# HGRN heads: state increments of a direction in a row into two PSUM banks, then the states, then the products with the states

## The chip, the cores and the metric

The kernel runs on one core of one Trainium2 chip. The metric is the device time of one execution in microseconds (us); before the change three runs took 1531.09, 1536.82 and 1536.36 us, median 1536.36. About 0.5% (7.7 us) is what a measurement of this kernel can tell from no change.

## The reference, cut to what matters

The program is a two-layer encoder over 512 tokens of width 1024. The even layer projects its input, mixes half of the channels by a bidirectional gated linear recurrence (HGRN2, 4 heads of 128) and the other half by RWKV-7 (8 heads of 64), concatenates, projects out, and runs a convolutional feed-forward; the odd layer mixes by Fourier transforms and a convolution. Only the HGRN recurrence is touched. Per head and direction the reference computes, chunk after chunk:

```
def step(state, xs):
    q_n, k_n, v_n, dec_n = xs
    o_n = jnp.einsum('bchd,bhdv->bchv', q_n, state)
    state = state * dec_n[..., None] + jnp.einsum('bchd,bchv->bhdv', k_n, v_n)
    return state, o_n
_, o_inter = lax.scan(step, state0, xs)
return (o_intra + jnp.moveaxis(o_inter, 0, 1))
...
o = _gla_chunk_forward(q4, k_f, i4, lf_f) + flip(_gla_chunk_forward(flip(q4), flip(k_b), flip(i4), flip(lf_b)))
o = _rmsnorm(o, norm_g) * jax.nn.silu(heads(g))
```

The kernel cuts the 512 tokens into 8 chunks of 64. The increment of the state, the product of keys and values of one chunk, doesn't depend on the state; the next state and the product of queries with the state do.

## The kernel before

The even layer is a list of stages, PLAN (lines 53 to 64 of the kernel): for each pair p of RWKV heads `pair`, `unit0`, `unit1` (one for each direction), `inv0`, `inv1`, `chain0`, `chain1`, `post`; for each HGRN head `proj` (its part of the input projection) and `hgrn`; then `ada` (modulation vectors, products L207), and `out 0`, `out 1`, the parts of the output projection whose inputs are complete (blocks of nine 128x512 products, L136 to L138, added up by VectorE in L870). The last part of the output projection (L1058 to L1062, `ab_out2`) needs the results of the last HGRN head and of the last `post`.

Each unit of RWKV has a triangular solve on VectorE, 62 short instructions one after the other (L555, L557), on tiles that exist once (`L`, `xi`, lines 542 and 543); its result is copied by L601 and L602, goes to DRAM and back through SyncE's queue (L603, L612, L614), and is then used by `inv` (products L620, L630, L641, L647, additions L649) and `chain` (seven steps: two small products L658, a copy by VectorE L659, a copy by ScalarE L660; then sixteen products L666). There are eight units and so eight solves. `post` normalises the sum of the two directions: on VectorE L672, L681, L682, L684, L688, on ScalarE L686 and the logarithm and exponential behind L689, on VectorE L690, then PE's transposes L693, ScalarE's L695 and L698, PE's L702 and L706 with VectorE's L703, L704 and L707 between them. The last `post` ends in `split` (L147, L148), whose two parts feed the second half of the products of `ab_out2`.

In `hgrn` (from L750) the chunk loop L816 to L831 goes through n = 0 to 7 with both directions in turn: the product of queries with the state (L821) into the tile `O` in PSUM bank `o`, the increment (L825) into a tile of bank `h`, of which there is one, and the new state on VectorE (L828 for the first, L830 for the others), in two buffers per direction. An increment can't be written before VectorE has read the one before it out of bank `h`, whichever direction that was. Bank `o` is also used by the scores of the head (L789 to L794), its transposes (L746, L841) and by `post`.

The order of the instructions of an engine isn't the order of the code: the program is scheduled when it is built, by priorities (the third number of each entry of PLAN) in a simulated timeline, with each engine's queue in order afterwards. A change in one stage so moves instructions of all stages that run beside it. DMAs are all issued by SyncE in one queue.

Of the kernel before, what the change touches and what calls it, by code (L numbers as in the profile page):

```python
# [16 lines left out]
P = 128  # L17
T = 512
# [5 lines left out]
# Feature blocks of the input projection of the even layer that run while the input is modulated.  # L24
FIRST = (24, 32, 33, 20, 28, 34)
CD_ORDER = [4, 8, 5, 9, 6, 10, 7, 11, 0, 1, 2, 3]
# Rows of the output projection of the even layer (in blocks), in the order their inputs are complete.
# [4 lines left out]
# Columns of the table of per-feature vectors: (name, number of 128-wide columns).  # L32
# [13 lines left out]
# Order of the stages of the even layer, each with its head or pair of heads and its priority.  # L46
# [21 lines left out]
def encoder(ctx: ExitStack, tc: tile.TileContext, A, out, dbg=None):  # L68
# [82 lines left out]
    def modulate(t, x, rs, scale, shift):  # L151
        """Parts of x * rs * scale + shift."""
# [11 lines left out]
    def load_ln(after):  # L164
        """Loads the table set that has both Ln and Exp, once `after` has been issued."""
        with tc.high_priority(URGENT):
            pre = act.preload_act_table_set(LNEXP)
        tc.add_manual_dep(pre.ins, after.ins.name, NOSYNC, reason="table set")
        return pre.ins

    def ln_exp(dst, src, eps, scale, after):
        """dst = (scale * src + eps) ** -0.5"""
# [26 lines left out]
    def adaln(l, s, ch, tag):  # L199
        """Shift, scale or gate of one block, by the tensor engine."""  # L200
# [13 lines left out]
    def dot(w, row, dst):  # L214
        """The sums of w * row along the partitions of w, which is lost."""
        dve.scalar_tensor_tensor(w, w, 1.0, row, op0=ALU.mult, op1=ALU.mult, accum_out=dst)  # L216

    def sc_row(pool):
        """silu(c) on each partition."""
# [9 lines left out]
    def adaln_steps(l, s, chunks):  # L229
        """The same by the vector engine, as a sequence of small steps between other work."""  # L230
# [36 lines left out]
    def start():  # L267
        """Norm and modulation of the input block by block, as their weights arrive, together with the first
        products that need them."""
# [88 lines left out]
    # ================= layer 0 =================  # L358
    def layer0(ys):
# [22 lines left out]
        # 1 - mu0 - mu1 and 1 - ka  # L382
# [5 lines left out]
        # per chunk: the identity, and B and K of the unit at hand  # L388
# [4 lines left out]
        # masks of A itself and of its scores  # L393
# [5 lines left out]
        # HGRN lower bound: first row of the softmax over the layers  # L399
# [13 lines left out]
        # f = (lb + olb) + olb * tanh, 1 - f = olb - olb * tanh, with olb half of 1 - lb  # L413
# [33 lines left out]
        def rwkv_pair(p):  # L447
# [5 lines left out]
            # normalised kk  # L453
# [13 lines left out]
            # decays and gates of both directions, each on its half of the rows  # L467
# [676 lines left out]
```

## Time and profile before

| | |
|---|---|
| median of three runs | 1536.36 us (1531.09 to 1536.82) |
| profiled execution, span from the first to the last instruction | 1533.7 us |
| TensorE matmul (PE) busy | 1423.1 us, 93% |
| VectorE (DVE) busy | 1035.2 us, 67% |
| ScalarE (ACT) busy | 684.9 us, 45% |
| mean granted TensorE clock, share of full speed | 0.943 |
| increments L825 | 130 to 571 us, 56 products in 112 passes |
| products with the states L821 | 134 to 572 us, 56 products in 112 passes |

The profile gives no time for the profiled execution beyond its span. An f32 product shows as two passes (two instructions). "Clock" is the granted clock as a share of 2.4 GHz; 0.50 is its lower level, 1.2 GHz. The whole even-layer mixing lies between about 55 and 614 us, the four HGRN heads' chunk loops at 130 to 192, 317 to 374, 440 to 491 and 548 to 572 us, and the rest of the program behind it is not touched.

### The profile page before, as it was taken

The page shows a single profiled execution, that of the slowest core. Times are in us where ns is not written, and L with a number is a line of the kernel's source. Part 1 is how long each engine was busy: PE and PEld are TensorE (multiplying, and loading weights), DVE is VectorE, ACT ScalarE, POOL GpSimd, SP SyncE. Part 2 cuts the span into 40 slices and gives each one's busy share as a digit, 9 for nine tenths or more (in the row PEclk, how much of TensorE's full clock was granted, in tenths as well). Part 3 has the DMA queues.
Part 4 walks back from the last instruction along what each step waited for, and adds up shares of the span by engine and source line. Part 5 has one row for each costly group of instructions (what it writes and reads, how often), then busy time and mean ns, then how long its engine had stood idle before and what let it go on. Part 6 is the DMA issues. An engine that isn't in the chain of part 4 may idle for free.

```text
span 1533.7 us, 21743 instructions
## 1 busy us (share of the span) xinstructions
PE 1423.1 (93%) x8114; PEld 1109.3 (72%) x8114; DVE 1035.2 (67%) x2056; ACT 684.9 (45%) x1192; POOL 160.5 (10%) x224
## 2 busy tenths in 40 slices
PE   5998879999999998899999999998888999999996
PEld 3765656766767766688888888676756888888885
DVE  7679977697686857756566875679967653544544
ACT  4455444545544634543233243476555332332343
POOL 1030211101110000000000000069700000000000
PEclk8998878998997999999999999999899999999998
DMA  9211122332251443344544863222122332223222
GB/s 367 81 67 50 45 63 61 98 110 68 75 166 40 124 158 132 104 148 164 184 145 143 287 250 91 83 89 62 49 76 97 122 96 98 97 86 106 97 86 79
DMA packets 76282, 174.26 MB, mean 114 GB/s; under 512 B 28176, under 2 KB 33168, under 8 KB 75152
## 3 DMA queue, kind: packets, MB, share of 16 engines
q1 hardware_dynamic: 76176, 172.87, 34.4%
q8 instruction: 64, 1.05, 0.3%
q14 instruction: 42, 0.34, 0.1%
HBM read 166.02 MB, written 6.82 MB: 113 GB/s over the span
## 4 chain that ended last, share of the span: by engine, by line
PE 77%; DVE 10%; ACT 5%; DMA 3%; issue 3%; POOL 2%; SPq 1%; DVEq 0%; POOLq 0%; ACTq 0%
PE g L136 10%; PE g L137 10%; PE g L138 10%; PE c L136 6%; PE c L137 6%; PE c L138 6%; PE h L138 3%; PE h L137 3%; PE h L136 3%; PE o L136 3%; PE o L137 3%; PE o L138 3%; DVE wlo L131 2%; POOL nt L1014 1%; PE m L529 1%
## 5 line engine op out<-in xcount | busy, mean ns | idle before, releaser
L130 ACT CAST whi<-raw 128x512 fp32r<-128x512 f32 (+2 forms) x406 | 243.3, 604 | 521.6 <-PE g L137 197.7
L131 DVE TENSOR_TENSOR wlo<-raw,whi 128x512 fp32r<-128x512 f32 (+2 forms) x406 | 281.5, 697 | 185.7 <-ACT whi L130 184.7
L136 PE MATMUL g<-h,whi 128*128 128x512 f32 x620 | 255.8, 414 | 18.7 <-ACT h L156 8.5
L137 PE MATMUL g<-h,whi 128*128 128x512 f32 x620 | 251.4, 405 | 4.0 <-DVE h L157 4.0
L138 PE MATMUL g<-h,wlo 128*128 128x512 f32 x620 | 249.2, 402 | 4.6 <-DVE wlo L131 4.6
L136 PEld LDWEIGHTS g<-h,whi 128*128 128x128 f32 x620 | 120.6, 195 | 53.5 <-ACT h L156 11.2
L136 PE MATMUL c<-h,whi 128*128 128x512 f32 x334 | 133.8, 401 | 13.2 <-ACT h L156 6.0
L137 PEld LDWEIGHTS g<-h,whi 128*128 128x128 f32 x620 | 120.7, 195 | 34.0 <-DVE h L157 5.3
L138 PEld LDWEIGHTS g<-h,wlo 128*128 128x128 f32 x620 | 120.4, 194 | 34.4 <-DVE wlo L131 7.8
L138 PE MATMUL c<-h,wlo 128*128 128x512 f32 x334 | 132.9, 398 | 2.3 <-DVE wlo L131 2.3
L137 PE MATMUL c<-h,whi 128*128 128x512 f32 x334 | 133.5, 400 | 0.5 <-DVE h L157 0.5
L1014 POOL TENSOR_TENSOR nt<-nt,ta 128x512 f32<-128x512 f32 x60 | 87.7, 1473 | 3.9 <-ACT ta L1009 0.8
L136 PEld LDWEIGHTS c<-h,whi 128*128 128x128 f32 x334 | 64.7, 194 | 30.9 <-ACT h L156 7.6
L138 PEld LDWEIGHTS c<-h,wlo 128*128 128x128 f32 x334 | 64.5, 193 | 17.0 <-DVE wlo L131 3.6
L137 PEld LDWEIGHTS c<-h,whi 128*128 128x128 f32 x334 | 64.6, 194 | 14.9 <-DVE h L157 1.7
L216 DVE SCALAR_TENSOR_TENSOR ra<-ra,row 128x1024 f32<-128x1024 f32 x56 | 67.8, 1217 | 0.5 <-DMA ra<-ada 0.5
L555 DVE TENSOR_TENSOR tt<-L,xi 128x60 f32<-128x60 f32 (+24 forms) x248 | 55.8, 225 | 16.7 <-DMA L<-nd 10.6
L557 DVE TENSOR_TENSOR xi<-xi,tt 128x60 f32<-128x60 f32 (+24 forms) x248 | 53.8, 217 | 5.9
L137 PE MATMUL h<-h,whi 128*128 128x512 f32 x130 | 50.8, 391 | 0.0
L138 PE MATMUL h<-h,wlo 128*128 128x512 f32 x130 | 50.8, 391 | 0.0
L136 PE MATMUL h<-h,whi 128*128 128x512 f32 x130 | 50.8, 391 | 0.0
L136 PE MATMUL o<-h,whi 128*128 128x512 f32 x124 | 48.2, 389 | 0.0
(373 smaller groups left out, 2662.3 us busy)
## 6 DMA issues: line engine op xcount, KB each, us to landing
raw<-ffn_up SPq DMA_DIRECT2D x88, 512.0 KB, 3.3
ra<-ada SPq DMA_DIRECT2D x56, 512.0 KB, 3.8
raw<-ab_in SPq DMA_DIRECT2D x35, 512.0 KB, 3.4
raw<-ffn_down SPq DMA_DIRECT2D x32, 448.0 KB, 3.4
raw<-ada SPq DMA_DIRECT2D x24, 512.0 KB, 4.4
ada<-ada SPq DMA_DIRECT2D x8, 1024.0 KB, 10.7
raw<-ffn_down SPq DMA_DIRECT2D x16, 512.0 KB, 3.6
raw<-cd_in SPq DMA_DIRECT2D x12, 512.0 KB, 3.3
```

Source lines behind the costliest of these rows:

```text
L130: act.copy(hi[:, :n, :], raw[:, k0:k0 + n, :])
L131: dve.tensor_tensor(lo[:, :n, :], raw[:, k0:k0 + n, :], hi[:, :n, :].bitcast(F32), op=ALU.subtract)
L136: pe.matmul(ps, whi, xhi, start=first, stop=False)
L137: pe.matmul(ps, whi, xlo, start=False, stop=False)
L138: pe.matmul(ps, wlo, xhi, start=False, stop=last)
L216: dve.scalar_tensor_tensor(w, w, 1.0, row, op0=ALU.mult, op1=ALU.mult, accum_out=dst)
L529: pe.matmul(ps[hr, c, :], at[hr, c0 + c], ibk[hr, c0 + c].rearrange("p s t -> p (s t)"), start=True, stop=True)
L555: dve.tensor_tensor(tv, Lv[:, j + 1:, j:j + 1].broadcast_to([P, n, m]), xi[:, j:j + 1, :m].broadcast_to([P, n, m]), op=ALU.mult)
L557: dve.tensor_tensor(xi[:, j + 1:, :m], xi[:, j + 1:, :m], tv, op=ALU.add)
L1014: pl.tensor_tensor(pa, pa, tp, op=ALU.add)
```

## The change

For each direction of a head all seven increments are now issued together, chunks of even number into a tile of bank `h`, those of odd number into a tile of bank `o`; then VectorE makes the seven states, each in a buffer of its own (seven per direction instead of two); only then does `O` get its place in bank `o`, and the eight products inside the chunks and the fourteen with the states follow each other. Numbers of products and VectorE instructions are the same. The second direction's tiles take the places of the first's in both banks, and `O` takes that of the second's in bank `o`. The ten further state buffers take 5 KB of each SBUF partition; the space for descriptors of software DMAs, which this kernel has none of, is set to 2048 bytes. Apart from this the diff only drops comments.

```
-            O = mps([P, 4, P], "o")
-            for c in range(8):
-                ... (8 products am x it into O)
-            S = [None, None]
-            for n in range(8):
-                for d in range(2):
-                    c = n if d == 0 else 7 - n
-                    if n > 0:
-                        pe.matmul(O[cr, c // 2, :], qd[d][:, c * 64:c * 64 + 64], S[d], start=False, stop=(n == 7), ...
-                    if n < 7:
-                        ps = mps([P, P], "h")
-                        pe.matmul(ps, kt[d][cr, c // 2, :], it[cr, c // 2, :], start=True, stop=True)
-                        sn = mk(rp, [P, P], f"hS{d}", bufs=2)
-                        ... (copy, or S * gl + ps)
+            S = [[None] * 8, [None] * 8]
+            for d in range(2):
+                pss = [mps([P, 4, P], t) for t in "ho"]
+                for n in range(7):
+                    c = n if d == 0 else 7 - n
+                    cr = slice(64 * (c % 2), 64 * (c % 2) + 64)
+                    pe.matmul(pss[c % 2][:, c // 2, :], kt[d][cr, c // 2, :], it[cr, c // 2, :], start=True, stop=True)
+                for n in range(7):
+                    c = n if d == 0 else 7 - n
+                    ps = pss[c % 2][:, c // 2, :]
+                    sn = mk(rp, [P, P], f"hS{d}", bufs=7)
+                    if n == 0:
+                        dve.tensor_copy(sn, ps)
+                    else:
+                        dve.scalar_tensor_tensor(sn, S[d][n], gl[d][:, 1, c:c + 1], ps, op0=ALU.mult, op1=ALU.add)
+                    S[d][n + 1] = sn
+            O = mps([P, 4, P], "o")
+            for c in range(8):
+                ... (8 products am x it into O)
+            for n in range(1, 8):
+                for d in range(2):
+                    ... (product of qd with S[d][n] into O)
...
-    nc = bacc.Bacc("TRN2", target_bir_lowering=False, num_devices=1)
+    nc = bacc.Bacc("TRN2", target_bir_lowering=False, num_devices=1, dynamic_dma_scratch_size=2048)
```

What this moves is shown at three places. In the rows, a line is the line of the kernel, then the operation, and out<-in with running numbers; lines of the new kernel behind L809 are 7 higher (L841 is L848 there, L870 is L877), the increments L825 are L818, the states L828 and L830 are L824 and L826, the eight products L813 are L831, and the products with the states L821 are L837.

PE before, in the last HGRN head: `c` with numbers from 5744 are the steps of the last `chain1`.

```order
L658 MATMUL c_5744<-X_4578,sc_4375 64x64 x2
L825 MATMUL h_5946<-it_5371,hkt_1226_5887 128x128
L821 MATMUL o_5893<-hS_1246_5943,hqd_1215_5812 64x128
L658 MATMUL c_5749<-X_4578,sc_4375 64x64 x2
L825 MATMUL h_5951<-it_5371,hkt_1218_5842 128x128
L821 MATMUL o_5893<-hS_1248_5948,hqd_1223_5857 64x128
L658 MATMUL c_5754<-X_4578,sc_4375 64x64 x2
L825 MATMUL h_5956<-it_5371,hkt_1226_5887 128x128
L821 MATMUL o_5893<-hS_1250_5953,hqd_1215_5812 64x128
L658 MATMUL c_5759<-X_4578,sc_4375 64x64 x2
L825 MATMUL h_5961<-it_5371,hkt_1218_5842 128x128
```

In a row there now, behind the last product with a state:

```order
L837 MATMUL o_5909<-hS_1214_5905,hqd_1193_5827 64x128
L837 MATMUL o_5909<-hS_1206_5884,hqd_1185_5782 64x128
L837 MATMUL o_5909<-hS_1215_5907,hqd_1193_5827 64x128
L630 MATMUL c_5442<-wt_5439,ZT_5413 32x32 x16
L641 MATMUL c_5461<-an_4367,Z_5412 64x128 x8
L641 MATMUL c_5471<-an_4367,Z_5412 64x128 x8
L848 MATMUL o_5941<-ident_71,ht_5939 128x128 x4
L647 MATMUL c_5481<-brs_4501,an_4367 128x128 x4
L647 MATMUL c_5482<-brs_4501,an_4367 128x128 x4
L136 MATMUL g_6029<-h_6007,whi_6025 128x512
L136 MATMUL g_6046<-h_6007,whi_6042 128x512
```

The pairs of L825 and L821 between the steps of the chain are gone, and the steps of that chain (L658) no longer stand ahead of the blocks of `out 1` (L136 on `g`) but among and behind them.

PE before, in the last `post`: L693 stands among the blocks of `out 1` (tiles `g_6069` to `g_6188`), and so do L702 and L706, three and five blocks later.

```order
L138 MATMUL g_6069<-h_6059,wlo_6066 128x512
L137 MATMUL g_6086<-h_6060,whi_6082 128x512
L138 MATMUL g_6086<-h_6059,wlo_6083 128x512
L693 MATMUL o_6214<-ident_71,ot_6200 128x128 x4
L136 MATMUL g_6103<-h_6047,whi_6099 128x512
L137 MATMUL g_6103<-h_6048,whi_6099 128x512
```

Now, behind the eighth and last block of `out 1` (tile `g_6148`):

```order
L136 MATMUL g_6260<-h_5948,whi_6256 128x512
L137 MATMUL g_6260<-h_5949,whi_6256 128x512
L658 MATMUL c_5734<-X_4558,sc_4355 64x64 x2
L138 MATMUL g_6260<-h_5948,wlo_6257 128x512
L658 MATMUL c_5739<-X_4558,sc_4355 64x64 x2
L658 MATMUL c_5744<-X_4558,sc_4355 64x64 x2
L666 MATMUL c_5749<-X_4558,sc_4355 64x64 x16
L136 MATMUL c_6232<-h_5948,whi_6228 128x512
L137 MATMUL c_6232<-h_5949,whi_6228 128x512
L138 MATMUL c_6232<-h_5948,wlo_6229 128x512
L693 MATMUL o_6174<-ident_71,ot_6160 128x128 x4
L702 MATMUL o_6182<-kds_4140,bones_105 128x512
```

The last three steps of the chain, L666 and the three PE parts of the last `post` moved behind the last block of `out 1`; between L666 and L706 only three 128x512 products are left, and three more (`o_6246`) before the first that needs the result of `post` (`h_6189`).

VectorE before, in the last solve (tiles `L_4417`, `xi_4418`): L690 of the third pair's `post`.

```order
L555 TENSOR_TENSOR tt_4452<-L_4417,xi_4418 128x69
L557 TENSOR_TENSOR xi_4418<-xi_4418,tt_4452 128x23x3
L690 TENSOR_TENSOR ot_5714<-ot_5714,st_5722 128x512
L555 TENSOR_TENSOR tt_4455<-L_4417,xi_4418 128x66
L557 TENSOR_TENSOR xi_4418<-xi_4418,tt_4455 128x22x3
```

Now, at the end of the same solve (there `L_4397`, `xi_4398`):

```order
L555 TENSOR_TENSOR tt_4498<-L_4397,xi_4398 128x8
L557 TENSOR_TENSOR xi_4398<-xi_4398,tt_4498 128x8
L601 COPY L_4397<-xi_4398 32x256 x4
L690 TENSOR_TENSOR ot_5684<-ot_5684,st_5692 128x512
L824 COPY hS_1200_5872<-h_5863 128x128
L649 TENSOR_TENSOR sc_4132<-sc_4132,c_4895 128x512
L649 TENSOR_TENSOR sc_4132<-sc_4132,c_4896 128x512
L649 TENSOR_TENSOR sc_4132<-sc_4132,c_4907 128x512
```

L690 moved from the middle of the last solve to behind its copies L601, and all four additions L649 that the last `chain0` needs stand behind it; before, two of them stood ahead of L601 and two right behind. On PE the products of that `inv` (L630, L641, L647) and that chain's steps stood between the blocks of `proj 3` and `out 0`; now they stand behind the eighth block of `out 0`, as do the PE parts of the third pair's `post`.

## Rows read from the trace of the kernel before

**Rows 1.** Page, part 1: engines, busy us, share of the span, instructions.

```profile
PE 1423.1 (93%) x8114; PEld 1109.3 (72%) x8114; DVE 1035.2 (67%) x2056; ACT 684.9 (45%) x1192; POOL 160.5 (10%) x224
```

**Rows 2.** Busy time by stretch: us, sum of engines' busy, granted clock, DMA.

```profile
core 0: us, PE busy (x) PEld busy (x) DVE busy (x) ACT busy (x) POOL busy (x), PEclk, DMA share, GB/s
129.00:187.00 58.00, 51.24 (x407) 36.82 (x404) 52.81 (x171) 24.82 (x45) 9.04 (x18) 0.89 0.18 50
194.00:206.00 12.00, 5.40 (x26) 4.21 (x26) 5.06 (x16) 6.26 (x18) 0.00 (x0) 0.50 0.30 71
476.00:497.00 21.00, 20.09 (x136) 15.17 (x137) 11.42 (x46) 13.43 (x31) 0.73 (x5) 0.52 0.21 49
481.70:542.60 60.90, 59.94 (x381) 46.28 (x381) 46.08 (x133) 36.68 (x69) 3.77 (x9) 0.85 0.43 125
497.00:542.60 45.60, 45.21 (x270) 34.96 (x269) 39.18 (x108) 27.83 (x50) 3.04 (x4) 0.96 0.48 145
572.50:578.70 6.20, 2.19 (x37) 1.68 (x37) 4.70 (x11) 3.31 (x8) 0.00 (x0) 0.76 0.00 0
```

**Rows 3.** Line L825, until 480 us: what PE's idle time before it ended with.

```profile
L825 PEld LDWEIGHTS h<-it,hkt x78: 182/186/334, 129.8 to 478.5; 64*128 64x128 f32 x78
...
  DVE hS L830: 12.5, 10
```

**Rows 4.** Line L830: VectorE's idle time before it (whole program, then until 480 us).

```profile
L830 DVE SCALAR_TENSOR_TENSOR hS<-hS,gn,h x48: 316/340/349, 142.8 to 571.0; 128x128 f32<-128x128 f32 x48
...
  PE h L825: 9.6, 13
...
  PE h L825: 1.7, 2
```

**Rows 5.** Timeline, last head: PE's weight loads (start us, us).

```profile
556.91 0.29 PEld L825 LDWEIGHTS h<-it,hkt 64*128 64x128 f32 x2
557.32 0.19 PEld L821 LDWEIGHTS o<-hS,hqd 128*64 128x64 f32 x2
557.69 0.27 PEld L630 LDWEIGHTS c<-wt,ZT 32*32 32x32 f32 x12 [0.17 <-issue]
...
564.01 1.29 PEld L647 LDWEIGHTS c<-brs,an 64*128 64x128 f32 x14 [0.17 <-DVE sc L649]
```

**Rows 6.** Timeline: copies behind the last solve but one; a product row of `inv`.

```profile
480.13 1.57 DVE L601 COPY L<-xi 32x256 f32<-32x256 f32 x4
...
559.34 1.96 PE L641 MATMUL c<-an,Z 64*64 64x128 f32 x32
```

**Rows 7.** Timeline: the last `post` and its split.

```profile
575.33 0.68 DVE L672 TENSOR_TENSOR yy<-yy,c 128x512 f32<-128x512 f32 x1
576.04 0.74 DVE L681 TENSOR_REDUCE st<-yy 128x4 f32<-128x256 f32 x2
577.56 0.76 DVE L684 TENSOR_TENSOR ot<-yy,st 128x256 f32<-128x256 f32 x2
578.52 0.63 ACT L686 ACTIVATE ot<-ot 128x512 f32<-128x512 f32 x1
579.44 0.68 DVE L688 TENSOR_REDUCE st<-ot 128x8 f32<-128x512 f32 x1
582.23 0.69 DVE L690 TENSOR_TENSOR ot<-ot,st 128x512 f32<-128x512 f32 x1
584.71 0.60 PE L693 MATMUL o<-ident,ot 128*128 128x128 f32 x4
585.35 0.78 ACT L695 ACTIVATE ot<-o,cols 64x512 f32<-64x512 f32 x1 [0.16 <-PE o L693]
589.51 1.02 PE L702 MATMUL o<-kds,bones 128*128 128x512 f32 x2
598.55 0.62 ACT L147 CAST h<-ot 128x512 fp32r<-128x512 f32 x1 [0.73 <-PE g L137]
```

**Rows 8.** Timeline: products of `out 1` behind PE's idle time and later.

```profile
580.17 0.63 PE L138 MATMUL g<-h,wlo 128*128 128x512 f32 x1
580.60 0.63 PE L137 MATMUL g<-h,whi 128*128 128x512 f32 x1
...
582.63 0.39 PE L138 MATMUL g<-h,wlo 128*128 128x512 f32 x1
582.86 0.39 PE L137 MATMUL g<-h,whi 128*128 128x512 f32 x1
```

More of the change, by code (lines that the diff above doesn't have):

```diff
@@ L819, in hgrn @@
                     cr = slice(64 * (c % 2), 64 * (c % 2) + 64)
-                    if n > 0:
-                        pe.matmul(O[cr, c // 2, :], qd[d][:, c * 64:c * 64 + 64], S[d], start=False, stop=(n == 7),
-                                  skip_group_check=True)
-                    if n < 7:
-                        ps = mps([P, P], "h")
-                        pe.matmul(ps, kt[d][cr, c // 2, :], it[cr, c // 2, :], start=True, stop=True)
-                        sn = mk(rp, [P, P], f"hS{d}", bufs=2)
-                        if n == 0:
-                            dve.tensor_copy(sn, ps)
-                        else:
-                            dve.scalar_tensor_tensor(sn, S[d], gl[d][:, 1, c:c + 1], ps, op0=ALU.mult, op1=ALU.add)
-                        S[d] = sn
+                    pe.matmul(O[cr, c // 2, :], qd[d][:, c * 64:c * 64 + 64], S[d][n], start=False, stop=(n == 7),
+                              skip_group_check=True)
             sq = htmp([P, 4, P])
```

## The prediction

> **What bounds the kernel now.** I read the page first, for the engines' shares: PE is busy 93% of the span, VectorE 67% [rows 1], and the change removes no product. So a gain must come from PE's idle time, from time at the lower clock, or from products that take less when they stand together. Then the lines of the loop, for what is waited for: until 480 us PE sat idle 12.5 us before increments L825 because VectorE hadn't read the one before [rows 3]; in the last head it is VectorE that waits for L825, 9.6 us in all, 1.7 of it before 480 [rows 4], so 7.9 there. Then stretches of the trace around the heads, for which engine is full. In the first head's stretch, 129 to 187 us, VectorE is busy 52.8 of 58.0 us and PE 51.2: the solves pace it, and PE's waits are mostly slack [rows 2]. In 476 to 497 us, where the third head's loop runs beside a `chain1`, PE is busy 20.1 of 21.0 us by the record, but at a granted clock of 0.52, nearly all at the lower level, and VectorE only 11.4 us [rows 2]: both chains crawl. Behind it, 497 to 542.6 us, VectorE is busy 39.2 of 45.6 us (86%), at a clock of 0.96. At the end of the layer I read the timeline of the last `post`: from L672 at 575.33 to the split at 598.55 us [rows 7] its chain lies beside the blocks of `out 1`, so it costs PE little.
>
> **Products that stand together.** Alone, the weights of a pair of passes of L825 begin 0.41 us before those of the next (556.91 to 557.32), and of L821 0.37 us (to 557.69); fourteen passes in a row of L647, the nearest shape (64x128 weights, 128 columns), take 1.29 us, 0.092 a pass, 0.18 a product [rows 5]. So a product of L825 costs 0.23 us less in a row and one of L821 0.19, 14 of each 5.8 us a head; the rows come in about five pieces with 0.17 us of entry each [rows 5], so 5.0 us a head. VectorE's work stays: 14 states at 0.34 us [rows 4]. The price of the 20 us in four heads is what PE's time is worth in each stretch, so I take three.
>
> **Until 481.7 us** (heads 0 to 2, up to the copies behind the last solve but one [rows 6]). VectorE paces, and each solve has to end before the next begins. All 14 states of head 0 now stand within or ahead of the first solve, where 4 stood, so that solve ends up to 10 x 0.34 = 3.4 us later; the next loses as many instructions, but VectorE waited there anyway (5.1 of 12.0 us busy in 194 to 206 us [rows 2]). The bounds: 12.5 us gained, if every wait of [rows 3] was on the path, and 3.4 lost. I take 2 us lost, near the second, since VectorE and not PE is full there.
>
> **From 481.7 to 542.6 us.** The crawl goes: the third head's products stand in rows ahead of it, and the steps of that `chain1` between blocks of `proj 3` and `out 0`. What limits then is VectorE up to L690 of the third pair's `post`, which now follows the last solve. Before, VectorE is busy 46.1 us here [rows 2]. Up to L690 the new order leaves out four L649, L703, L704, four L659, three L830 and the three last VectorE steps of head 2's norm (together some 8.0 us at 0.69 us for each 128x512 operation, as L690 [rows 7], and 0.2 to 0.34 for the small), and adds one L870, three L659 and the four operations L568, L571 and L575 (4.5 us): 42.6 us. At this stretch's own density, 46.1 of 60.9, that takes 56.3 us, 4.6 less; at the 86% of 497 to 542.6 us, 49.5 us, 11.4 less; at 100%, 18.3 less. I take the middle of the first two, 8 us gained, because steps of `chain1` that PE reaches late will make VectorE wait in its queue.
>
> **From there to the end of the layer.** Moved in from ahead: L630 (32 passes at 0.27/12, 0.7 us), L641 (1.96 us [rows 6]), sixteen L647 (32 passes at 0.092, 2.9), five steps L658 (0.37 each by the hand-overs of [rows 5], 1.9), L693 and L702 (0.6 and 1.0 [rows 7]): 9.1 us. Of these about 5 us stand ahead of L693, while PE waits for L690, and cost nothing; if PE has no such wait, all 9.1 count. So +4.1.
>
> Uncovered: the last `post`. Its chain is L672 0.68, L681 0.74, L684 0.76, L686 0.63, from L688's start to L690's 2.79 (with the table load of the logarithm), L690 0.69, then L693 0.60, two of L695 1.56, L702 1.02, L703 0.69 (as L690), L706 as L702 1.02, L707 0.69, L147 0.62 [rows 7]: 12.5 us, and ten hand-overs at 0.2 us (L684 ends 578.32, L686 starts 578.52 [rows 7]), 14.5 us. L693, L702 and L706 are work in either kernel (2.6 us). Before, six of the eight blocks of `out 1` lie between L693 and the split, and the first two ahead of L693; now six products lie beside the whole chain, 0.23 us each from start to start [rows 8], 1.4 us. So PE stands idle 14.5 - 2.6 - 1.4 = 10.5 us more. The steps of the last chain that stand behind the last block wait for VectorE and ScalarE, about 1 us. Against this the last head's rows save 5.0, and of the 4.0 us that PE stands idle in 572.5 to 578.7 us, before the blocks [rows 2], I take half, since L630 and L641 now lie beside that head's norm.
>
> The idle time has a second price. After the 6.2 us in which PE was busy 2.2, at a clock of 0.76 [rows 2], products started 0.43 us apart (580.17, 580.60), and 0.23 apart from 582.63 [rows 8]; so after a longer gap the rest of `ab_out2` starts at the lower level too. I take eight or nine products, 9 x 0.20 = 1.8 us, as in that stretch. The sum here: 4.1 + 10.5 + 1.0 + 1.8 - 5.0 - 2.0 = 10.4 us lost. Bounds: 3.4 us lost, if the rows give back VectorE's 7.9 us of waits [rows 4] instead of 5.0 and the 4.1 us hide as well; 21.4 lost, if none of the 9.1 us hides (5.0 more) and all products left of `ab_out2`, 48 less 9, start at the lower level (30 x 0.20, 6.0 more).
>
> **The waits that are added.** The second direction's increments wait for the first's seven states (7 x 0.34, 2.4 us), and `O` for the second's; behind them stand steps L658, L666 or blocks. In heads 0 to 2 the order puts other products between; in head 3 three steps of a chain, so it is inside the sum. On SyncE the last solve's round trip now stands among loads for `ada`; L620, which needs it, stands behind the whole last `chain0`, which covers it. The SBUF setting adds no instruction.
>
> **Sum.** 2 - 8 + 10.4 = 4.4 us on the profiled 1533.7, so 1538.1. The profile's span is 2.7 us under the median 1536.36, and I add that: 1541. The rest of the program has the same order but for a few swaps.
>
> **Rivals.** *The clock stays down at the end* (slower). The price: all 39 products left of `ab_out2` 0.43 us apart instead of 0.23, 6 us beyond the 1.8, and behind PE's thin stretch in the last head 17 products of `out 1` too (3.4 more): 1541 + 9.4 = 1550. It decides from a clock of 0.50 through the last 8 us of `ab_out2`. For it, 194 to 206 us: busy 5.4 of 12.0, clock 0.50 all along [rows 2]. Against it, [rows 8], where it came back in 4 us.
>
> *Rows keep the clock and the waits were on the path* (faster). The 12.5 us of [rows 3] are gained instead of 2 lost, and the second stretch runs at 86% (3.4 more): 1541 - 14.5 - 3.4 = 1523. For it, the 0.52 in 476 to 497 us, where single products alternated with waits. The Trainium skill, "TensorE: Matmul & The Clock Gate", section "HAM oscillation — how this bites in real kernels", has it that products in bursts with waits between them fall back to the lower rate, so gathering them would pay. By that rule alone the time would be this rival's. The trace agrees at 194 to 206 us, and not plainly at 476 to 497 us, where PE's record is 96% busy and the clock half nevertheless [rows 2]. Against the rival: VectorE's 91% in the first stretch, and that the same rule also speaks of the gap at the end.
>
> *It doesn't do what it says.* PE's queue had other products for most of its waits, and the second and third stretch cancel: 8 us gained there, and in the last stretch as much lost (10.4 with half of the 4.1 hidden), the first unchanged: 1536. For it, PE's 93% [rows 1]; against it, that the last `post` has nothing beside it.
>
> **Chances.** Forecast 0.45 (its own range 1533 to 1549), slower rival 0.25, faster rival 0.15, no effect 0.15. No change is 1528.7 to 1544 (0.5%, about what a measurement can tell): two thirds of the forecast, all of no effect, a fifth of the faster and a tenth of the slower rival, together 0.51; a bit over a quarter of the forecast and the rest of the slower rival make slower 0.34; what is left, faster 0.15. The range takes in both rivals but for their outer halves: 1526 to 1556.
>
> **What would show it.** Right: no idle time before increments, solves that end within 3 us of their times before until 482, L690 of the third `post` right behind the last solve at 532 to 538 us with a clock near 1 ahead of it, and PE idle 8 to 12 us between the last L666 and the second half of `ab_out2`. Wrong would be a first stretch that gives back the 12.5 us, a clock of 0.5 beside the rows of increments, or a last `post` that lies beside products after all. A time below 1526 or above 1556 would mean that solves moved by more than their instructions.

## The result and the profile after

The changed kernel takes 1543.26 us (median of five runs, 1541.46 to 1546.45); the kernel before, in five runs, 1532.76 (1530.51 to 1536.82). The ratio is 1.0056 [1.0037, 1.0075]: slower, by about what the text on record called the least that can be told, 0.5%. The forecast was 1541; "slower" had a chance of 0.34 there. The band that the prediction called no change, 1528.7 to 1544, hung on the median of 1536.36 and still holds 1543.26; against the kernel before as it is timed now, the change is 10.5 us where 4.6 were forecast. The profiled execution has a span of 1542.4 us, 8.7 more than before, where the sum had 4.4. The time is inside the range given, but the terms of the sum don't come out, and this is what the rest is about.

Page, part 1, of the changed kernel [rows 1]:

```profile
PE 1412.1 (92%) x8114; PEld 1101.8 (71%) x8114; DVE 1035.0 (67%) x2056; ACT 684.1 (44%) x1192; POOL 163.6 (11%) x224
```

PE is recorded as busy 11.0 us less, and the kernel is 8.7 us longer. Five marks show where (us); each is the start of one instruction, but for the 542.6, which is a place in VectorE's order before the change, not its L690 (that stood at 500.09):

| mark | before | after | difference |
|---|---|---|---|
| L601, copies behind the last solve but one | 480.13 | 475.27 | -4.9 |
| L690 of the third `post` (before: the place that the prediction took for it) | 542.6 | 524.94 | -17.7 |
| last sum of the even layer (L1062, now L1069) | 614.62 | 619.51 | +4.9 |
| fourth sigmoid of the odd layer (L924, now L931) | 1030.37 | 1035.72 | +5.4 |
| last L319 of the odd layer's first output part | 1152.47 | 1161.30 | +8.8 |

So 17.7 us are gained up to 525 us, 22.6 are lost between there and the end of the even layer, and 3.5 more in the odd layer, which the change doesn't touch. Products that moved from ahead of the second mark to behind it are in both of the first two numbers; their sum, 4.9 us lost in the even layer, doesn't depend on the place taken. Busy time by stretch in the changed kernel, to be read against [rows 2] (columns as there):

```profile
core 0: us, PE busy (x) PEld busy (x) DVE busy (x) ACT busy (x) POOL busy (x), PEclk, DMA share, GB/s
129.00:187.00 58.00, 48.21 (x398) 34.72 (x394) 47.75 (x150) 29.51 (x50) 8.60 (x18) 0.84 0.19 55
476.00:497.00 21.00, 20.02 (x163) 16.01 (x154) 15.75 (x53) 14.43 (x31) 0.74 (x5) 1.00 0.41 103
475.30:524.90 49.60, 48.39 (x425) 37.49 (x427) 42.82 (x127) 31.43 (x65) 4.50 (x7) 1.00 0.54 161
524.90:619.50 94.60, 78.24 (x596) 56.05 (x588) 48.99 (x103) 32.24 (x69) 0.60 (x2) 0.84 0.30 99
543.00:553.00 10.00, 10.00 (x120) 8.91 (x120) 2.60 (x8) 1.52 (x4) 0.00 (x0) 0.51 0.01 2
590.00:612.00 22.00, 14.23 (x37) 8.92 (x38) 10.48 (x20) 9.24 (x16) 0.00 (x0) 0.69 0.29 106
```

The crawl at 476 to 497 us is gone: the clock there is 1.00 where it was 0.52, with PE as busy as before. But the half clock is back at 543 to 553 us, beside the last head's own rows, and again at 590 to 612, in and behind the last `post`. There PE's waits are the ones that the order foretold (timeline; the bracket is the idle time before an instruction and what ended it):

```profile
587.59 1.15 PE L666 MATMUL c<-X,sc 128*64 128x64 f32 x32 [0.31 <-DVE X L659]
594.56 1.11 PE L693 MATMUL o<-ident,ot 128*128 128x128 f32 x4 [4.93 <-DVE ot L690]
597.33 2.08 PE L702 MATMUL o<-kds,bones 128*128 128x512 f32 x2 [1.65 <-ACT ot L698]
600.18 2.08 PE L706 MATMUL o<-gd,lg 128*128 128x512 f32 x2 [0.78 <-DVE kds L703]
603.04 0.80 PE L136 MATMUL o<-h,whi 128*128 128x512 f32 x1 [0.78 <-DVE ot L707]
603.63 0.63 PE L137 MATMUL o<-h,whi 128*128 128x512 f32 x1
604.06 0.63 PE L138 MATMUL o<-h,wlo 128*128 128x512 f32 x1
...
608.49 0.40 PE L137 MATMUL h<-h,whi 128*128 128x512 f32 x1
608.72 0.39 PE L136 MATMUL c<-h,whi 128*128 128x512 f32 x1
...
614.67 0.55 PE L136 MATMUL c<-h,whi 128*128 128x512 f32 x1 [2.14 <-ACT whi L130]
615.01 0.63 PE L137 MATMUL c<-h,whi 128*128 128x512 f32 x1
```

The four waits make 8.1 us, L702 and L706 take 2.08 us each where [rows 7] has 1.02, twelve products behind them start 0.43 us apart, and after one more wait of 2.14 us, for weights, nine more do (614.67 to 618.00).

What the change set out to remove is removed. The wait of PE for VectorE, 12.5 us in ten places [rows 3], is down to 0.2 us in one place for the increments, now L818; eight passes in a row load in 0.96 us; and of VectorE's wait for increments [rows 4] 2.4 us are left:

```profile
L818 PEld LDWEIGHTS h<-it,hkt x56: 182/188/331, 130.5 to 545.2; 64*128 64x128 f32 x56
...
  issue: 1.3, 4
  PE c L658: 0.8, 1
  DVE X L659: 0.7, 1
  ACT X L660: 0.4, 1
  DVE xi L557: 0.4, 1
  DVE an L531: 0.3, 1
  DVE hS L826: 0.2, 1
```

```profile
523.28 0.96 PEld L818 LDWEIGHTS h<-it,hkt 64*128 64x128 f32 x8 [0.17 <-issue]
```

```profile
L826 DVE SCALAR_TENSOR_TENSOR hS<-hS,gn,o x24: 329/342/348, 133.9 to 547.7; 128x128 f32<-128x128 f32 x24
...
  PE h L818: 1.8, 1
  PE o L818: 0.6, 1
```

### The profile page after: what moved, and what is told of

The parts are those of the page before. It is cut to its first block, busy times and chain, and to the rows that moved or that the text cites. A ratio compares the mean times of both kernels' runs of the same rounds, so it can differ in the third digit from the quotient of the medians.

```text
span 1542.4 us, 21736 instructions
## 1 busy us (share of the span) xinstructions
PE 1412.1 (92%) x8114; PEld 1101.8 (71%) x8114; DVE 1035.0 (67%) x2056; ACT 684.1 (44%) x1192; POOL 163.6 (11%) x224
## 4 chain that ended last, share of the span: by engine, by line
PE 72%; DVE 13%; ACT 6%; issue 4%; DMA 3%; SPq 1%; POOL 0%; DVEq 0%; ACTq 0%; POOLq 0%
PE g L136 9%; PE g L137 9%; PE g L138 9%; PE c L136 6%; PE c L137 6%; PE c L138 6%; PE h L136 3%; PE h L137 3%; PE h L138 3%; PE o L136 3%; PE o L137 3%; PE o L138 3%; DVE wlo L131 2%; DVE h L1027 2%; PE m L529 1%
## 5 line engine op out<-in xcount | busy, mean ns | idle before, releaser
L131 DVE TENSOR_TENSOR wlo<-raw,whi 128x512 fp32r<-128x512 f32 (+2 forms) x406 | 282.6, 700 | 189.0 <-ACT whi L130 173.4
L136 PE MATMUL g<-h,whi 128*128 128x512 f32 x620 | 253.4, 409 | 14.7 <-ACT h L156 8.3
L136 PEld LDWEIGHTS g<-h,whi 128*128 128x128 f32 x620 | 119.9, 194 | 46.9 <-ACT h L156 10.4
L136 PE MATMUL c<-h,whi 128*128 128x512 f32 x334 | 134.1, 402 | 15.2 <-ACT h L156 6.0
L136 PEld LDWEIGHTS c<-h,whi 128*128 128x128 f32 x334 | 64.4, 193 | 32.4 <-ACT h L156 7.6
L138 PEld LDWEIGHTS c<-h,wlo 128*128 128x128 f32 x334 | 64.4, 193 | 15.1 <-DVE wlo L131 1.6
L136 PE MATMUL h<-h,whi 128*128 128x512 f32 x130 | 51.1, 393 | 0.0
L136 PE MATMUL o<-h,whi 128*128 128x512 f32 x124 | 49.2, 397 | 0.8 <-DVE ot L707 0.8
```

The costliest lines, as they stand in the source:

```text
L131: dve.tensor_tensor(lo[:, :n, :], raw[:, k0:k0 + n, :], hi[:, :n, :].bitcast(F32), op=ALU.subtract)
L136: pe.matmul(ps, whi, xhi, start=first, stop=False)
L138: pe.matmul(ps, wlo, xhi, start=False, stop=last)
```

## The experiments

All were timed in five rounds beside the kernel before. "Layer" is the start of the even layer's last sum in the profile, "odd" the time from the fourth sigmoid to the last L319 of the odd layer's first output part; the edits don't touch the odd layer, and its instructions are the same in all of them; only the order that the scheduler gives it differs.

| run | median us | ratio to before | layer | odd |
|---|---|---|---|---|
| before (profile) | 1532.76 | | 614.62 | 122.10 |
| changed kernel | 1543.26 | 1.0056 [1.0037, 1.0075] | 619.51 | 125.58 |
| loop_allocation_only | 1534.50 | 1.0001 [0.9986, 1.0016] | 613.56 | 121.92 |
| rows_heads01 | 1538.16 | 1.0018 [1.0004, 1.0032] | 612.13 | 125.51 |
| rows_head2 | 1529.51 | 0.9965 [0.9947, 0.9982] | 612.40 | 120.52 |
| rows_head3 | 1542.78 | 1.0051 [1.0031, 1.0070] | 624.39 | 120.83 |
| rows_heads012 | 1535.35 | 1.0007 [0.9990, 1.0025] | 619.45 | 118.29 |
| rows_all_post_covered | 1542.40 | 1.0040 [1.0016, 1.0064] | 625.69 | 125.55 |
| all_rows_hold1 | 1537.03 | 1.0018 [1.0002, 1.0035] | 615.88 | 119.10 |
| all_rows_hold2 | 1539.77 | 1.0064 [1.0039, 1.0089] | 615.48 | 125.58 |
| all_rows_hold | 1529.66 | 0.9974 [0.9957, 0.9991] | 614.64 | 118.31 |
| head2_hold3 | 1531.50 | 0.9995 [0.9972, 1.0018] | 602.46 | 125.12 |
| head2_hold | 1526.00 | 0.9942 [0.9921, 0.9962] | 608.25 | 119.18 |
| head2_hold5 | 1523.14 | 0.9948 [0.9928, 0.9968] | 605.53 | 118.31 |

A position is one execution's: where the order is the same word for word, the first solve ended at 149.46 us before the change and at 147.10 in loop_allocation_only, and the layer 1.1 us apart; over all seven kernels that keep the loop in heads 0 and 1 the first solve ends at 146.95 to 150.19. Lengths between marks repeat better (from the solve before the last to the end of the layer, 134.49 us in both). A profiled execution can also lie away from the median of its kernel: that of rows_all_post_covered took 1549.97 us, the slowest of twelve (1533.66 to 1549.97), that of head2_hold3 1524.43, the fastest of twelve (to 1540.56).

**Which heads.** The new rows for some heads (the tuple is `(0, 1)`, `(2,)`, `(3,)`, `(0, 1, 2)` or, for the allocation alone, empty), the loop with the new allocation for the others:

```
+            if h in (0, 1):
                 S = [[None] * 8, [None] * 8]
                 ...
+            else:
+                O = mps([P, 4, P], "o")
+                ...
```

> Only heads 0 and 1 have their increments in a row; heads 2 and 3 keep the loop (with seven state buffers per direction). The blocks of `out 1` again stand beside the last `post`, as before the change, and the half-clock crawl at 476 to 497 us should be back. The order behind the even layer is word for word that of the changed kernel. My theory (three stretches): the solves of heads 0 and 1 end 2 to 8 us late, as in the changed kernel, nothing is gained at 482 to 542 us, nothing is lost at the end: the even layer ends 2 to 6 us later than before, the time is 1535 to 1539 us. If the 3.8 us that the changed kernel loses behind 620 us also come from the order there, 4 us more: 1539 to 1543. Rival (PE's waits before the increments were on the path): 8 us less than before, 1525.

> Only head 2 has its increments in a row; everything ahead of it keeps the order of the kernel before. The last `post` has no block of `out 1` beside it here either, though head 3 keeps the loop. My theory: the clock near 1.0 in 476 to 497 us, L690 of the third `post` 10 to 14 us earlier than before, then the uncovered last `post` (PE idle 7 to 12 us in it) and the moved-in products, 10 to 14 us lost: the even layer ends within 3 us of before, and with up to 4 us from the order behind it 1532 to 1540 us. Rival (head 3's rows are what costs at the end, the place of the blocks is not): the gain stays, 1521 to 1525. Rival (rows at head 2 do not bring the clock back): 1540 to 1548.

> Only head 3 has its increments in a row; the order up to the end of head 2 is that of the kernel before, and the last `post` stands uncovered behind the last block of `out 1`. My theory: the crawl at 476 to 497 us at a clock near 0.5 stays, nothing is gained up to 542 us, and the end loses what it lost in the changed kernel, less the products that moved in there from ahead (4 us): 6 to 11 us, with up to 4 us from the order behind the layer: 1539 to 1548 us, the slowest of the four. Rival (the rows of head 3 save PE 5 us and VectorE its 7.9 us of waits there, and the post is no loss): 1525 to 1530. Rival (the loss in the changed kernel comes from heads 0 to 2): 1531 to 1534, as before.

> Rows in heads 0, 1 and 2; head 3 keeps the loop. The difference to the changed kernel is head 3 alone (and the odd layer's order, that of the kernel with rows in head 3). My theory now: the rows of head 3 cost the most, since the clock falls to half beside them (0.67 in 540 to 560 us) where the loop of the last head kept 1.00, with the products of other work between its pairs: up to L690 of the third `post` as in the changed kernel (524 to 526 us), then a clock of 0.95 or more in 540 to 560 us, the even layer ends 5 to 8 us earlier than in the changed kernel, 1529 to 1534 us. Rival (the loss at the end comes with the late solves of heads 0 and 1 and with the uncovered `post`, whatever head 3 does): the layer ends as in the changed kernel, 1537 to 1541 us.

> The loop of the kernel before in all heads, with the changed kernel's allocation alone: seven state buffers per direction and the descriptor space of 2048 bytes. Every engine's order is that of the kernel before. My theory: no effect, 1531 to 1537 us, each solve's end and the ends of both layers within 1 us of the profile before. Rival (the allocation itself, or chance between executions, moves the time): solves or the 1030 to 1150 us stretch move by 3 us or more.

The allocation does nothing to the time, as expected, and nothing to the odd layer. Its solves don't end within the 1 us expected, though: the sixth ends 4.0 us earlier than before (399.60 to 403.56), by more than the rival's 3, with every order the same. Since the time and the length from the solve before the last are the same, this is put down to chance between executions; single positions are read with it. Rows in head 2 alone make the kernel faster, though its last `post` is uncovered: the clock stays at 1.00 where the crawl was (476 to 497 us) and on through the last head, and is low in the last `post`:

```profile
540.00:560.00 20.00, 17.79 (x244) 14.31 (x243) 9.44 (x23) 8.51 (x20) 0.00 (x0) 1.00 0.09 26
580.00:600.00 20.00, 11.32 (x55) 6.37 (x56) 6.90 (x14) 6.13 (x12) 0.00 (x0) 0.68 0.07 23
```

The layer ends 2.2 us ahead of before, within the 3 expected. The median, 1529.51, is below the range given: the order of the odd layer gains 1.6 us there where up to 4 of loss were allowed for, and the profiled execution, at 1532.38, is itself 2.9 us above the median. Rows in head 3 alone keep the crawl (a clock of 0.51 in 476 to 497 us) and cost 9.8 us at the layer's end, as expected. Rows in heads 0 and 1 contradict the expectation, though the time, 1538.16, is inside its range, by the 3.4 us of the odd layer's order: their solves end 3 to 12 us late up to 404 us, and yet the solve before the last ends 2.1 us early (478.06) and the layer 2.5 us early, with the crawl only partly back (a clock of 0.69 in 478 to 500 us). What makes up for the late solves was not tried by an edit, but the traces show where it lies: from the sixth solve to the seventh it takes 70.00 us in place of 76.57, and 22 products of 128x512 that stood behind the sixth solve's end now start ahead of it (5.1 us at 0.23 each).

rows_heads012 refuted the theory that I had by then, that head 3's rows cost the most. With the loop back in head 3 the layer ends at 619.45, as in the changed kernel; by length, from the solve before the last, it takes 147.84 us against 144.24, so that head 3's rows rather save a little beside the others. (The time, 1535.35, is lower than the rival's by the odd layer's order.) Its stretch from 534 to 558 us:

```profile
534.00:558.00 24.00, 23.78 (x268) 18.74 (x270) 6.33 (x22) 3.41 (x13) 0.00 (x0) 0.50 0.15 48
```

Half clock for 24 us, with PE recorded as 99% busy, beside the loop. And in rows_head3, with the last head in rows, the clock doesn't fall:

```profile
540.00:560.00 20.00, 20.00 (x325) 13.65 (x324) 10.79 (x29) 5.12 (x13) 0.00 (x0) 1.00 0.65 226
```

So it isn't the form of the last head that decides. In all six kernels with rows in heads 0, 1 and 2 together the clock falls to the lower level at the last head, between 533 and 544 us, and in none of the eight others. Which products stand beside the last head doesn't decide either: in the changed kernel, in rows_heads012 and in rows_head2 they are the last steps of the last `chain0` (L658, L666) and products of the last `inv1` (L620 to L641), and in rows_head2 the clock stays at 1.00. In the 9 us ahead of the fall (534 to 543 us) PE was busy 6.16 us in the changed kernel and 7.35 us in rows_heads012 (525.2 to 534.2 us); in rows_head2, where it didn't fall, 7.52 us from 534 to 543. What makes the difference is open.

**The last `post`.** First by priorities in PLAN, then by holding the last blocks of `out 1` behind the last L666 on PE (its instruction, `end`, is kept in `rwkv_chain`; `o >= 4` is all_rows_hold, 6 and 7 are all_rows_hold2 and all_rows_hold1):

```
-    ("chain0", 3, 0), ("inv1", 3, 1000), ... ("chain1", 3, 12100),
+    ("chain0", 3, 15000), ("inv1", 3, 16000), ... ("chain1", 3, 20100),
```

```
+            ends[q["p"], d] = end.ins
...
-                gemm(ps, w, yy, len(yy))
+                with (tc.issue_after(ends[3, 1]) if i == 1 and o >= 4 else nullcontext()):
+                    gemm(ps, w, yy, len(yy))
```

> The changed kernel with the priorities of three entries of PLAN raised (`inv1 3` 1000 to 16000, `chain0 3` 0 to 15000, `chain1 3` 12100 to 20100), so that 39 products of `out 1` and `ab_out2` stand between the last L666 and L693 where 3 stood; 3 and 1 stand between L693, L702 and L706. Computation and instructions are the same. My theory (the uncovered last `post` is the loss): PE idle in it falls from 7.8 to 2 or 3 us and the products behind it run at the full clock: 6 to 9 us less than the changed kernel, 1534 to 1538 us. Rival (the last head's chain is bound by VectorE whatever stands beside it): 1541 to 1545, unchanged.

> The changed kernel, with the last four blocks of `out 1` put behind the last L666 on PE, so that they stand beside the last `post` (27 products between L666 and L693, 12 between L693 and L702, 3 before L706; 3, 0 and 0 in the changed kernel). All that stands ahead is instruction for instruction as in the changed kernel; the order in the odd layer is the one of the kernel with rows in head 3 alone, not the changed kernel's. My theory (the uncovered last `post` was 8 us of idle time and half-clock products): the even layer ends 5 to 8 us earlier than in the changed kernel, that is 3 us before to level with the kernel before; with the other order in the odd layer 5 us more: 1530 to 1534 us. Rival (the blocks are only moved, and the steps of the last `chain1` stand idle in their place): the even layer ends as in the changed kernel, 1537 to 1540 us, by the odd layer's order alone. If neither counts: 1543.

> The changed kernel with only the last two blocks of `out 1` behind the last L666; the order in the odd layer is again word for word the changed kernel's. My theory (the uncovered `post` costs what it stands idle, and the odd layer's order costs 3.5 us between 1030 and 1150 us on its own): the even layer ends 2 to 4 us earlier than in the changed kernel, the odd layer loses its 3.4 to 3.5 us as in the changed kernel: 1538 to 1541 us. Rival (the order in the odd layer is of no account, its differences are chance): the stretch from the fourth sigmoid to the last L319 of the first output part takes what it takes in the kernel before, 122.1 us, within 1 us, and the time is 1535 to 1537.

> The changed kernel with only the last block of `out 1` behind the last L666; the order in the odd layer is that of the kernel with rows in head 2. My theory: the even layer ends 0 to 2 us earlier than in the changed kernel (less than with two blocks), but the stretch in the odd layer is 1.5 to 3 us shorter than before instead of 3.5 longer: 1536 to 1539 us, and not above the kernel with two blocks moved, though less of the `post` is covered. Rival (the odd layer's order is of no account): 1 to 3 us above the kernel with two blocks moved.

The priorities settle nothing: PE's waits in the last `post` fell to 2.5 us, as expected, but solves moved too (the fifth ends 5.8 us later than in the changed kernel), 540 to 560 us ran at a clock of 0.56, and this profile is the slowest of its kernel. The held blocks do: all ahead of them is the changed kernel's order, PE waits 0.78 us before `ab_out2` in place of 8.1 in all, and from the solve before the last the layer takes 140.35 us where the changed kernel takes 144.24. So covering the `post` is worth 3.9 us, less than the 5 to 8 expected. Of the 7.3 us of waits that went, 3.4 came back at PE's next wait, which was 2.14 us in the changed kernel (614.67) and is 5.53 now:

```profile
596.30 0.50 PE L136 MATMUL o<-h,whi 128*128 128x512 f32 x1 [0.78 <-DVE ot L708]
609.12 0.80 PE L136 MATMUL c<-h,whi 128*128 128x512 f32 x1 [5.53 <-ACT whi L130]
```

(the weights of the last blocks of `ab_out2`). With two blocks held it is 141.60 us, with one 145.30, nothing gained.

Of the rest of what all_rows_hold gains, 1543.3 to 1529.7, the odd layer has 7.3 us (125.58 to 118.31); the last 2.4 us lie elsewhere. Holding one block gave a better time than holding two, ratio 1.0018 against 1.0064, as the theory of the odd layer's order said, with 119.10 us there against 125.58.

**Head 2 with the held blocks.** The same two edits, rows in head 2 alone, three, four or five blocks held:

> Rows in head 2 alone, with the last four blocks of `out 1` behind the last L666 in the same way; the order ahead and the order of the odd layer are those of the kernel with rows in head 2. There the last `post` ran with PE idle 8.7 of 20 us at a clock of 0.68. My theory: 4 to 7 us less than with rows in head 2 alone, 1523 to 1526 us. Rival (the blocks are only moved): 1528 to 1531, no difference.

> Rows in head 2 alone, the last three blocks of `out 1` behind the last L666 (four in the kernel that took 1526.0); the order in the odd layer is word for word that of the changed kernel. My theory: the even layer ends within 2 us of where it did with four blocks (608.3 us), the stretch in the odd layer is 3.4 us longer than before (2.9 shorter there): 1530 to 1533 us. Rival (the odd layer's order is of no account): 1525 to 1528.

> Rows in head 2 alone, the last five blocks of `out 1` behind the last L666; the order in the odd layer is that of the kernel with all rows and four blocks moved (3.8 us shorter than before there). My theory: the even layer ends within 2 us of the kernel with four blocks (608.3 us), since the two gaps share the same products, and the odd layer gains another 1 us: 1524 to 1527 us, the fastest or level with 1526.0. Rival (the steps of the last `chain1`, with fewer products between them, come earlier by what they no longer queue): 2 to 4 us less, 1522 to 1524.

head2_hold and head2_hold5 beat both kernels (0.9942 and 0.9948, not to be told apart). Holding four blocks gained 3.5 us on rows_head2, a little less than the 4 to 7 expected; from the solve before the last it is 130.83 us in place of 134.54, 3.7 less, close to the 3.9 of all_rows_hold. With five the time is in the rival's range, but its layer ends 2.7 us earlier than with four, and 2.3 of that already stood at the solve before the last, so nothing speaks for the rival. With three blocks, and the changed kernel's order in the odd layer, it is 0.9995, inside the range that went with that order, though its even layer ended earlier than that of either (602.46 us in the profiled execution, 5.8 us ahead of head2_hold, of which 4.9 already stood at the solve before the last). The odd layer's marks in the changed kernel and in head2_hold5:

```profile
1035.72 0.59 ACT L931 ACTIVATE sq<-g 128x512 f32<-128x512 f32 x1
1124.00 0.69 DVE L1030 TENSOR_TENSOR acc<-acc,nt 128x512 f32<-128x512 f32 x1
1127.27 2.48 DVE L1040 SCALAR_TENSOR_TENSOR acc<-m,acc 128x512 f32<-128x512 f32 x4 [2.57 <-PE m L1037]
1161.30 0.75 DVE L319 SCALAR_TENSOR_TENSOR x<-g,mod,x 128x512 f32<-128x512 f32 x1 [0.52 <-PE g L138]
```

```profile
1019.23 0.58 ACT L958 ACTIVATE sq<-g 128x512 f32<-128x512 f32 x1
1101.54 0.67 DVE L1057 TENSOR_TENSOR acc<-acc,nt 128x512 f32<-128x512 f32 x1
1103.43 2.48 DVE L1067 SCALAR_TENSOR_TENSOR acc<-m,acc 128x512 f32<-128x512 f32 x4 [0.62 <-PE m L1064]
1137.54 0.75 DVE L319 SCALAR_TENSOR_TENSOR x<-g,mod,x 128x512 f32<-128x512 f32 x1 [0.52 <-PE g L138]
```

VectorE's last addition of the convolution (L1030, L1057 in the second) comes 88.3 us behind the sigmoid in the one and 82.3 in the other, and the norm, whose first VectorE instruction is the third row, waits for it. Up to there VectorE is full in both, 87.21 of 88.28 us and 80.66 of 82.31:

```profile
1035.72:1124.00 88.28, 74.33 (x322) 59.16 (x321) 87.21 (x108) 49.47 (x86) 71.89 (x50) 0.90 0.21 66
```

```profile
1019.23:1101.54 82.31, 71.27 (x322) 55.79 (x320) 80.66 (x103) 48.46 (x85) 71.16 (x49) 0.96 0.21 62
```

So VectorE has 6.6 us more to do between the two marks in the changed kernel: five instructions, three steps of the convolution (L1027) and two of the weights' splits (L131), that the other order does outside this stretch, and some that take longer.

Four orders of this layer came up in the fourteen kernels. The changed kernel's gave 125.12 to 125.58 us in five of them, that of the kernel before 122.10 and 121.92, a third 119.10, 119.18 and 120.52, a fourth 118.29, 118.31, 118.31 and 120.83. The third and the fourth have the same order on VectorE and ScalarE and their times overlap, so they aren't told apart; the first two are clear of each other and of these.

## Why the prediction was right or wrong, point by point

| step | predicted | measured in the profile |
|---|---|---|
| heads 0 to 2, to the solve before the last | +2 (-12.5 to +3.4) | -4.9 |
| from there to L690 of the third `post` | -8 (-18.3 to -4.6 by VectorE's density) | -12.8 |
| from there to the end of the even layer | +10.4 (3.4 to 21.4) | +22.6 |
| behind it | 0 | +0.5 and +3.5 |

**The rows.** Right in kind, too large for head 3: 0.96 us for eight passes gives 0.11 a pass after the first (0.092 assumed), and in head 3 most of the rows ran at the half clock, in the stretch from 543 to 553 us above. Behind the solve before the last, PE's time less idle time less what the clock took (the length times one less the clock) is 111.9 us before (134.49, 9.14 idle, clock 0.90) and 110.8 after (144.24, 17.58 idle, 0.89): 1.1 us less work, not 5 (the clock, given to two digits, leaves about 0.7 us either way in each). Of the 9.8 us by which this length grew, idle time has 8.4 and the clock 2.4 (15.9 against 13.4): what the crawl gave back was lost again further on.

```profile
480.13:614.62 134.49, 125.35 (x966) 93.56 (x964) 92.50 (x229) 67.18 (x133) 3.77 (x9) 0.90 0.41 131
```

```profile
475.27:619.51 144.24, 126.66 (x1017) 93.57 (x1015) 91.84 (x230) 63.69 (x133) 5.10 (x9) 0.89 0.38 120
```

The same count gives 111.1 for rows_head2 (134.54, 16.69 idle, 0.95), 111.8 for head2_hold5 (130.43, 12.15, 0.95) and 109.5 for rows_heads012 (147.84, 17.69, 0.86). Which heads have rows hardly changes the work behind this solve; idle time and clock make the length. Between rows_head2 and the changed kernel, 9.7 us, it is the clock (6.7 against 15.9).

**Until 482 us.** "VectorE paces" failed as a price for all three heads. Up to the sixth solve the kernel lost, as the sum had it: the first solve ended 3.8 us late, as the 3.4 said, the fifth 11.9, the sixth 5.1 (it ends at 405.6 to 408.9 us in the six kernels with rows in heads 0 and 1 and the same priorities, at 399.6 to 403.6 in the seven with the loop there). PE's waits before the increments went, but PE stood idle 59.9 us up to the sixth solve's end where it had been 54.2, so the rival's 12.5 us weren't on the path: 10.5 of them stood in head 0, 2.0 in head 1 and none from 400 to 480 us. Whether VectorE alone paced there isn't shown, since it was busy 47.75 of 58.0 us in the first stretch now, 52.81 before. What was made up, 10.0 us, lies between the sixth solve and the seventh, where the third head's loop runs (before and after):

```profile
403.56:480.13 76.57, 71.21 (x744) 51.80 (x743) 60.13 (x159) 32.80 (x70) 6.80 (x13) 0.98 0.38 109
```

```profile
408.66:475.27 66.61, 60.75 (x665) 44.37 (x663) 57.00 (x155) 32.74 (x63) 7.65 (x13) 0.97 0.43 128
```

Here it is PE that is full, 93% and 91%, idle 5.4 and 5.9 us, and its busy time fell by 10.5. All six kernels with rows in heads 0 to 2 take 64.9 to 66.6 us for it, the three with the loop in these heads 76.6 to 79.5. So the step that failed is that the first head's stretch in [rows 2] was read as the bound of all three. How much of the 10 us the rows save and how much is products that moved out of the stretch wasn't separated.

**The crawl.** Right, and larger: clock 1.00, L690 at 524.94, ahead of the 532 to 538 given. VectorE was busy 42.82 of 49.60 us up to it, the 42.6 of the sum, at 86%, the denser of the two densities, where I took the middle. The Trainium skill's rule that the rival cited ("TensorE: Matmul & The Clock Gate", "HAM oscillation — how this bites in real kernels") agrees with the last `post`, where PE waited 4.93 us ahead of L693 and the half clock came back. At 476 to 497 us the outcome is the rule's, but not its condition: PE stood idle only 0.91 of 21.0 us there before the change. It doesn't settle the fall at 543 us: PE was idle 2.84 of the 9 us ahead of it, 1.65 ahead of the fall in rows_heads012, and 1.48 in rows_head2, which didn't fall.

**The end.** The step that failed most. Two of its terms were right: PE's waits in the last `post`, 8.1 us where the sum had 10.5 and the signs 8 to 12, and the products at the lower level behind a gap. Mis-sized was the clock: 1.8 us was taken for nine products; measured over 524.9 to 619.5 us it is 15.1 (94.6 at 0.84) against 3.6 in the stretch of the kernel before that answers to it (72.0 at 0.95), 11.5 more:

```profile
542.60:614.60 72.00, 63.84 (x580) 46.25 (x578) 44.87 (x94) 28.98 (x61) 0.00 (x0) 0.95 0.40 139
```

Besides the nine, twelve more products, L702 and L706 at twice their time, and ten microseconds at 0.51 beside the last head's rows, which no term had. (Counted so, the clock's share takes in idle time at the lower level.) Idle time is 16.4 against 8.2 us, 8.2 more of the 22.6. What is left, 2.9 us, is products moved in, less what the rows save. Of the 7.9 us of VectorE's waits that the lower bound counted on in the last head, 1.2 stood in the third head's loop, between 480 and 500 us. The rival "the clock stays down at the end" had the kind of loss but not its place: its last 8 us weren't at 0.50 (0.77 from 612.0).

**Behind it.** "The rest of the program has the same order but for a few swaps" failed: the few swaps are worth 3.5 us of the 8.7. In the three profiles with the changed kernel's odd order and other even layers (rows_heads01, all_rows_hold2, rows_all_post_covered) it is 125.5 to 125.6 us as well, and 125.1 in head2_hold3, so it isn't chance.

**The sum.** 4.4 was forecast and 8.7 came, within the range because errors of -6.9, -4.8 and +12.2 in the three stretches almost cancel. This was luck and not the mechanism: a crawl that goes in one place and comes in another was counted as a gain, and the odd layer's order as nothing.

## What to carry to other kernels

Chains that wait for other engines need products that fill their gaps. Here the rows moved those products: the last `post` was left with 8.1 us of waits and the lower clock behind them, and a low-clock stretch that went in one place came back in another. So take the row where the clock is low and other work stands ready (head 2 here: 0.35% faster alone, of which about a third is the odd layer's order, and 0.5 to 0.6% with four or five blocks of `out 1` kept for the last `post`), not everywhere. Read for each stretch which engine is full: VectorE's share in the first head's stretch told nothing of the third's. And where a scheduler orders the program, compare the order of the parts that weren't touched, above all where an engine is full: here the same instructions in another order took 118.3 to 125.6 us.

## What the runs showed of the hardware that was not expected

The granted clock stood at 0.50 to 0.52 in stretches in which the record has PE almost wholly busy: 20.09 of 21.0 us before the change [rows 2], 10.00 of 10.0 at 543 to 553 us after it, 23.78 of 24.0 in rows_heads012. In rows_head2 the last head's products ran at 1.00 with PE busy 17.79 of 20.0, in rows_head3 at 1.00 with 20.00 of 20.0. PE's busy share so doesn't tell the clock; it has to be read for each stretch.
